# PEER trunk: exponential of the picks written one step later, one-hot compare on pairs, some splits and modulation rows given to GpSimd

## The chip, the cores and the metric

The kernel runs on one core of a Trainium2 chip. The metric is device time in microseconds (us) of one execution; the time before is a median of three runs.

## The reference, cut to what matters

Two layers; each has a mixer (causal pooling beside sliding-window attention) and then an expert network (PEER), both with a norm scaled and shifted by a modulation `mod = silu(c) @ w_ada + b_ada`. T = 256 tokens, D = 1024, 8 heads, 128 x 128 experts, 16 of them picked per token and head:

```python
def peer_ffn(h, wq, subkeys, u, v):
    q = (hf @ wq).reshape(T, PEER_HEADS, 2, D_HALF)
    s = jnp.einsum('thpd,pnd->thpn', q, subkeys)
    top_s, top_i = lax.top_k(s, PEER_TOPK)                       # 16 of 128, twice per head
    cand = top_s[:, :, 0, :, None] + top_s[:, :, 1, None, :]
    best_s, best_j = lax.top_k(cand.reshape(T, PEER_HEADS, 256), PEER_TOPK)
    i1 = jnp.take_along_axis(top_i[:, :, 0], best_j // PEER_TOPK, axis=-1)
    i2 = jnp.take_along_axis(top_i[:, :, 1], best_j % PEER_TOPK, axis=-1)
    expert = i1 * N_KEYS + i2
    gate = jax.nn.softmax(best_s, axis=-1)
    act = gelu(h . u[expert]) * gate
    return act @ v[expert]
```

## The kernel before

The experts are computed densely: every row of U and V is read once per layer, and a gate matrix of zeros and gates, built on chip from the picks, weighs the activations. Weights are float32 and come as tiles of 128 x 1024 (512 KB). Each is split into two float16 parts: ScalarE writes the high part, `activation(hi, r, Copy, scale)` (L86), and VectorE the low part, `r * scale - hi`, in one operation with two inputs (L87). Per layer the expert network reads 16 tiles of wq, 128 tiles of U and 128 of V, in this order.

`Stream` holds the order of all tiles. SP's queue issues the loads (L81), nine tiles ahead of use, into a pool "raw" of five buffers, so that a load waits until a split has freed its buffer; the splits run three tiles ahead, into a pool "hl" of five buffers.

A tile of U is 24 matmuls of 128x256 (`mm_u`, L309): for each of eight slices hi x hhi, hi x hlo, lo x hhi. Two tiles (a pair) fill a PSUM tile "mm", of which there are two buffers, and ScalarE empties it with one Gelu (L828). TensorE can therefore run two pairs ahead of the Gelu.

The generator `picks()` (L672 to L754) yields 68 steps per layer. The loops over the wq tiles and over the first 32 pairs of U tiles call `next(pick)` in between, some two steps per pair. All steps are VectorE's but for one exponential and one copy on ScalarE and four transposes per token tile on TensorE. In order:

- 48 top-16 searches (L666 to L670: MAX8, FIND_INDEX8, MATCH_REPLACE8, MAX8, FIND_INDEX8), and the candidates between them;
- the softmax of the picked scores: the subtraction of the largest (L706), and on ScalarE the Exp (L707), which needs a table load, as does the Gelu behind it;
- integer arithmetic on the candidate numbers (L710 to L723) and the gates' split (L725 to L731);
- for each of two token tiles and two index halves a one-hot compare of 128x2048 float16 (L736), a product (L740) and four halving adds (L744, L746); then the transposes (L752) and the copy (L753).

Modulation rows: `ada_step` reads a 128x1024 tile of w_ada from the same stream, and VectorE multiplies it by a column of `cond` and adds it to `acc_a` (L287; the first row of eight by L285). In layer 0, 24 of them stand between the U tiles, one about every five tiles from tile 12 on.

The program's order is laid down per engine by a scheduler when the kernel is built: each engine runs its instructions in the order listed, so an instruction that waits holds up all behind it on its engine. In the names below `rawt` is a raw tile, `hlt` a split one (its number tells instances apart), `act` the big resident tile that holds the picks' work areas too.

Of the kernel before, what the change touches and what calls it, by code (L numbers as in the profile page):

```python
# [23 lines left out]
L = 2  # L24
# [21 lines left out]
class Arena:  # L46
    """Hands out column ranges of one float32 tile."""
# [15 lines left out]
class Stream:  # L63
    """Weight tiles [128, 1024] in the order of their use; loads and splits run ahead.  An item with a
    fourth field is loaded into a buffer of the splits."""

    def __init__(self, nc, items, raw, hl, ahead_dma, ahead_conv):
# [4 lines left out]
        self.dma_ins = []  # L72
        self.rt, self.ct = {}, {}
# [11 lines left out]
    def split(self, r, scale, hi, lo):  # L85
        self.nc.scalar.activation(hi, r, AF.Copy, scale=scale)  # L86
        self.nc.vector.scalar_tensor_tensor(lo, in0=r, scalar=scale, in1=hi, op0=ALU.mult,  # L87
                                            op1=ALU.subtract)

    def _conv(self, upto):  # L90
        while self.ncv <= min(upto, self.limit, len(self.items) - 1):
# [10 lines left out]
    def get(self, kind):  # L102
        """The next tile: (hi, lo), or the raw tile where the item has no scale."""
# [17 lines left out]
def trunk(ctx, tc, ins, out):  # L121
# [56 lines left out]
    def spread(main, bg, lo, hi):  # L178
        """bg spread evenly between main[lo:hi]."""
# [48 lines left out]
    def rsqrt(out_ap, ss_ap, scale, n):  # L228
        """out = 1/sqrt(ss*scale + EPS): exp(-ln/2), and a Newton step for float32's accuracy."""
# [740 lines left out]
```

## Time and profile before

| quantity | value |
|---|---|
| median of 3 runs | 1781.52 us (1780.1 to 1783.76) |
| profiled execution, first to last instruction | 1780.2 us |
| TensorE matmul busy | 1705.0 us (96%) |
| VectorE busy | 1436.6 us (81%) |
| ScalarE busy | 852.5 us (48%) |
| GpSimd busy | 29.2 us (2%) |
| DMA read | 360.78 MB, 203 GB/s over the span |

Busy time is a sum over instructions of the profiled execution, and the shares are averages over the whole span; the stretch of the picks lies between some 150 and 310 us in layer 0 and 1020 and 1170 us in layer 1. The profile records that execution's own time as its span, 1780.2 us; the runs that give the median were taken apart from it.

### The profile page before, as it was taken

Reading aid. Unit: us, or ns where it says so; the run is one execution under the profiler, and the core shown is the slowest. Engines: PE = TensorE matmul, PEld = TensorE weight load, DVE = VectorE, ACT = ScalarE, POOL = GpSimd, SP = SyncE. Lnnn points to the kernel's source line nnn. Section 1 sums busy time; section 2 is a strip of 40 time slices with the busy share of each in tenths; the row PEclk is TensorE's granted clock in tenths of the full one; section 3 lists DMA queues with packets and bytes.
Section 4 is the critical chain, followed back from the end, with each engine's and each line's share of the span. In section 5 each row is a group of like instructions: output and inputs, shape, how many; then the busy total and the mean of one; then the engine's idle time right before and its main releaser. Section 6 shows DMA issues by size and latency. Waiting matters only on the chain.

```text
span 1780.2 us, 33654 instructions
## 1 busy us (share of the span) xinstructions
PE 1705.0 (96%) x13524; PEld 1212.5 (68%) x13524; DVE 1436.6 (81%) x2587; ACT 852.5 (48%) x1146; POOL 29.2 (2%) x26
## 2 busy tenths in 40 slices
PE   4999989999999999999999998999999999999998
PEld 3758868999997455444458697888999845454443
DVE  6797999578889999877867499945888899986664
ACT  3645544544444444445656353545444444445543
POOL 0210000000000000000000000000000000000000
PEclk9989999999999999999999999999999999999999
DMA  8773456776665555778844144565555555556773
GB/s 315 285 277 120 168 196 220 264 241 207 222 220 187 187 190 199 257 259 314 315 155 154 36 152 163 180 220 201 187 181 188 186 181 183 185 189 213 227 227 126
DMA packets 100190, 364.04 MB, mean 204 GB/s; under 512 B 11680, under 2 KB 11696, under 8 KB 99648
## 3 DMA queue, kind: packets, MB, share of 16 engines
q1 hardware_dynamic: 99648, 361.29, 59.0%
q8 instruction: 106, 1.74, 0.4%
q0 software_dynamic: 384, 0.58, 0.1%
q14 instruction: 52, 0.43, 0.1%
HBM read 360.78 MB, written 1.05 MB: 203 GB/s over the span
## 4 chain that ended last, share of the span: by engine, by line
PE 81%; DVE 13%; DMA 2%; ACT 2%; issue 2%; SPq 0%; DVEq 0%; ACTq 0%
PE acc L327 38%; PE mm L309 34%; DVE hlt L87 4%; PE g L778 2%; PE g L780 2%; DVE act L670 1%; DVE act L668 1%; DVE act L667 1%; DVE act L669 1%; PE acc L319 1%; DMA rawt<-in_wq_dram 1%; DVE act L666 1%; DMA rawt<-in_adar_dram 1%; PE acc L516 1%; PE g L554 1%
## 5 line engine op out<-in xcount | busy, mean ns | idle before, releaser
L309 PE MATMUL mm<-hbuf,hlt 128*128 128x256 f16 x6816 | 767.5, 273 | 20.6 <-ACT act L828 11.1
L86 ACT ACTIVATE hlt<-rawt 128x1024 f16<-128x1024 f32 x544 | 571.4, 1052 | 439.9 <-PE acc L327 179.9
L87 DVE SCALAR_TENSOR_TENSOR hlt<-rawt,hlt 128x1024 f16<-128x1024 f32 x544 | 660.9, 1219 | 122.5 <-ACT hlt L86 117.9
L309 PEld LDWEIGHTS <-hlt 128*128 128x128 f16 x6816 | 662.8, 98 | 102.3 <-DVE hlt L87 13.4
L327 PE MATMUL acc<-hlt,hbuf 128*128 128x512 f16 x3072 | 674.4, 379 | 5.4 <-ACT hbuf L853 5.4
L327 PEld LDWEIGHTS <-hbuf 128*128 128x128 f16 x3264 | 314.9, 98 | 379.8 <-ACT hbuf L853 5.9
L828 ACT ACTIVATE act<-mm 128x512 f32<-128x512 f32 x128 | 76.4, 597 | 174.4 <-PE mm L309 174.4
L853 ACT ACTIVATE hbuf<-act 128x512 f16<-128x512 f32 x128 | 79.0, 626 | 101.4 <-PE acc L327 101.1
L287 DVE SCALAR_TENSOR_TENSOR acc_a<-rawt,cond,acc_a 128x1024 f32<-128x1024 f32 x59 | 75.6, 1282 | 51.1 <-DMA rawt<-in_adar_dram 50.8
L854 DVE TENSOR_TENSOR hbuf<-act,hbuf 128x512 f16<-128x512 f32 x128 | 87.7, 689 | 31.8 <-ACT hbuf L853 31.8
L768 DVE TENSOR_TENSOR lt<-iot,pk 128x1024 f16<-128x1024 f16 x128 | 87.5, 684 | 1.4 <-ACT pk L753 1.4
L783 DVE TENSOR_TENSOR act<-act,g 128x512 f32<-128x512 f32 x128 | 87.0, 680 | 1.7 <-PE g L780 1.7
L774 DVE TENSOR_TENSOR rl<-rt,pk 128x512 f16<-128x512 f16 x128 | 53.8, 421 | 33.7 <-PE g L780 33.1
L778 PE MATMUL g<-rl,lt 128*128 128x64 f16 x1024 | 78.3, 193 | 0.0
L780 PE MATMUL g<-rh,lt 128*128 128x64 f16 x1024 | 78.2, 193 | 0.0
L778 PEld LDWEIGHTS <-lt 128*128 128x128 f16 x1024 | 71.1, 97 | 8.0
L780 PEld LDWEIGHTS <-lt 128*128 128x128 f16 x1024 | 66.3, 97 | 8.0
L87 DVE SCALAR_TENSOR_TENSOR act<-rawt,act 128x1024 f16<-128x1024 f32 x36 | 46.7, 1305 | 19.8 <-ACT act L86 19.8
L770 DVE TENSOR_TENSOR rt<-iot,pk 128x512 f16<-128x512 f16 x128 | 54.2, 424 | 3.9
L86 ACT ACTIVATE act<-rawt 128x1024 f16<-128x1024 f32 x36 | 37.7, 1058 | 39.9 <-DMA rawt<-in_win_dram 31.8
L773 DVE TENSOR_TENSOR rh<-rt,pk 128x512 f16<-128x512 f16 x128 | 53.5, 418 | 0.1
L309 PE MATMUL mm<-hbuf,act 128*128 128x256 f16 x384 | 47.1, 276 | 0.0
(182 smaller groups left out, 911.0 us busy)
## 6 DMA issues: line engine op xcount, KB each, us to landing
rawt<-in_u_dram SPq DMA_DIRECT2D x256, 512.0 KB, 3.9
rawt<-in_v_dram SPq DMA_DIRECT2D x256, 512.0 KB, 3.9
rawt<-in_adar_dram SPq DMA_DIRECT2D x88, 512.0 KB, 4.4
rawt<-in_wq_dram SPq DMA_DIRECT2D x32, 512.0 KB, 4.6
rawt<-in_win_dram SPq DMA_DIRECT2D x20, 512.0 KB, 4.9
rawt<-in_wout_dram SPq DMA_DIRECT2D x16, 512.0 KB, 5.1
hlt<-in_adar_dram SPq DMA_DIRECT2D x8, 512.0 KB, 7.6
act<-in_msk_dram SPq DMA_DIRECT2D x2, 1024.0 KB, 7.9
```

Of the source, the lines that this page charges most:

```text
L86: self.nc.scalar.activation(hi, r, AF.Copy, scale=scale)
L87: self.nc.vector.scalar_tensor_tensor(lo, in0=r, scalar=scale, in1=hi, op0=ALU.mult, op1=ALU.subtract)
L287: last["ada"] = dve.scalar_tensor_tensor(acc, in0=wt, scalar=sc, in1=acc, op0=ALU.mult, op1=ALU.add).ins
L309: pe.matmul(pt, lhsT=a[:, k], rhs=b[:, k], start=n == 0, stop=n == 23)
L327: last["mm"] = pe.matmul(acc[h], lhsT=a, rhs=b[:, h * 512:(h + 1) * 512], start=first and n == 0, stop=end and n == 2).ins
L768: dve.tensor_tensor(out=lt, in0=iot.unsqueeze(1).to_broadcast([P, 4, 128, 2]), in1=pv[0].to_broadcast([P, 4, 128, 2]), op=ALU.is_equal)
L778: pe.matmul(g3[:, t], lhsT=lt[:, t // 2, :, t % 2], rhs=rl[:, t // 2, :, t % 2], start=True, stop=False)
L780: pe.matmul(g3[:, t], lhsT=lt[:, t // 2, :, t % 2], rhs=rh[:, t // 2, :, t % 2], start=False, stop=True)
L783: dve.tensor_tensor(out=av, in0=av, in1=g3.rearrange("p t i -> p i t"), op=ALU.mult)
L828: act_e.activation(act[:, ip_ * 512:(ip_ + 1) * 512], pt, AF.Gelu, scale=1.0 / WS)
L853: tabs.append(act_e.activation(ahi, src, AF.Copy))
L854: dve.tensor_tensor(out=alo, in0=src, in1=ahi, op=ALU.subtract)
```

## The change

Four edits, told in the order of the diff.

1. `Stream.on_pool` names tiles whose low part is made elsewhere: wq tiles 6, 10, 14 and U tiles 2, 6, ... 58 of each layer. For these ScalarE writes the high part as before, then scales the raw tile in place (L89 of the new file), and GpSimd subtracts (L90). VectorE has no part in them.
2. `ada_step` is called with `pool` in the first 32 pairs: ScalarE scales the row's tile (L291 of the new file), GpSimd adds it to `acc_a` (L293); the first row of eight is ScalarE's alone.
3. The two index rows `jh` are written twice as wide, each value twice, so that the compare reads pairs of equal values against pairs of `iot16`, with two packed elements as the innermost step.
4. The Exp is written behind the first compare instead of right behind the subtraction, and the gates' split behind the first token tile's loop.

```diff
+        self.on_pool = set()
...
-    def split(self, r, scale, hi, lo):
+    def split(self, r, scale, hi, lo, pool=False):
         self.nc.scalar.activation(hi, r, AF.Copy, scale=scale)
+        if pool:
+            self.nc.scalar.activation(r, r, AF.Copy, scale=scale)
+            self.nc.gpsimd.tensor_tensor(out=lo, in0=r, in1=hi, op=ALU.subtract)
+            return
...
-                self.split(self.rt.pop(i), scale, hi, lo)
+                self.split(self.rt.pop(i), scale, hi, lo, i in self.on_pool)
...
     st = Stream(nc, items, raw, hl, 9, 3)
+    for kind, rng in (("w", range(6, 16, 4)), ("u", range(2, 60, 4))):
+        at = [i for i, t in enumerate(items) if t[2] == kind]
+        for l in range(L):
+            mine = at[l * len(at) // L:(l + 1) * len(at) // L]
+            st.on_pool |= {mine[n] for n in rng}
...
-            jh = [a.f(256, F16).rearrange("p (h r) -> p h r", h=16) for _ in range(2)]
+            jh = [a.f(512, F16).rearrange("p (n t) -> p n t", t=2) for _ in range(2)]
...
-            act_e.activation(gt, gt, AF.Exp)
             yield
...
-            dve.tensor_tensor(out=jh[0].rearrange("p h r -> p (h r)"), in0=t2, in1=s4, op=ALU.add)
+            twice = [v.unsqueeze(2).to_broadcast([P, 256, 2]) for v in (t2, s4)]
+            dve.tensor_tensor(out=jh[0], in0=twice[0], in1=twice[1], op=ALU.add)
...
-            dve.tensor_tensor(out=jh[1].rearrange("p h r -> p (h r)"), in0=t2, in1=s4, op=ALU.add)
+            dve.tensor_tensor(out=jh[1], in0=twice[0], in1=twice[1], op=ALU.add)
...
-                    j4 = jh[s][:, tt * 8:tt * 8 + 8]
-                    dve.tensor_tensor(out=o1, in0=j4.unsqueeze(3).to_broadcast([P, 8, 16, 16]),
-                                      in1=iot16.unsqueeze(1).unsqueeze(1).to_broadcast([P, 8, 16, 16]),
+                    j4 = jh[s][:, tt * 128:tt * 128 + 128]
+                    dve.tensor_tensor(out=o1.rearrange("p h r (c t) -> p (h r) c t", t=2),
+                                      in0=j4.unsqueeze(2).to_broadcast([P, 128, 8, 2]),
+                                      in1=iot16.rearrange("p (c t) -> p c t", t=2).unsqueeze(1).to_broadcast(
+                                          [P, 128, 8, 2]),
                                       op=ALU.is_equal)
                     yield
+                    if tt == 0 and s == 0:
+                        act_e.activation(gt, gt, AF.Exp)
...
+                if tt == 0:
+                    gate_split()
+                    yield
...
-                    ada_step(pg)
+                    ada_step(pg, pool=ip_ < 32)
```

`gate_split` holds the five lines of the gates' split, unchanged. The number of picks' steps stays 68.

ScalarE's order around the Exp of layer 0. In the order of before, mm_2254 is the Gelu of pair 7, and hlt_2354 and hlt_2395 are the high parts of U tiles 20 and 21:

```order
L828 ACTIVATE act_73<-mm_2178 128x512
L86 ACTIVATE hlt_2319<-rawt_2138 128x1024
L86 ACTIVATE hlt_2348<-rawt_2179 128x1024
L828 ACTIVATE act_73<-mm_2254 128x512
L86 ACTIVATE hlt_2354<-rawt_2185 128x1024
L86 ACTIVATE hlt_2395<-rawt_2214 128x1024
L707 ACT_TABLE_LOAD
L707 ACTIVATE act_73<-act_73 128x256
L828 ACT_TABLE_LOAD
L828 ACTIVATE act_73<-mm_2316 128x512
```

In the order now, mm_2114 is the Gelu of pair 5 (L848), rawt_2077 is a modulation row, rawt_1977 is U tile 14 being scaled in place for GpSimd, and hlt_2194, hlt_2223 and hlt_2290 are the high parts (L87) of U tiles 15, 16 and 17:

```order
L291 ACTIVATE rawt_2077<-rawt_2077,cond_84 128x1024
L89 ACTIVATE rawt_1977<-rawt_1977 128x1024
L87 ACTIVATE hlt_2194<-rawt_2006 128x1024
L848 ACTIVATE act_73<-mm_2114 128x512
L87 ACTIVATE hlt_2223<-rawt_2048 128x1024
L87 ACTIVATE hlt_2290<-rawt_2115 128x1024
L756 ACT_TABLE_LOAD
L756 ACTIVATE act_73<-act_73 128x256
L848 ACT_TABLE_LOAD
L848 ACTIVATE act_73<-mm_2184 128x512
```

The Exp (L707, now L756) moved from behind pair 7's Gelu to behind pair 5's, though it is written later; in layer 1 it moved from pair 6 to pair 5.

VectorE's order behind the Exp of layer 0, at the first compares. Before, hlt_2634 to hlt_2708 are the low parts of U tiles 27 to 30:

```order
L87 SCALAR_TENSOR_TENSOR hlt_2634<-rawt_2460,hlt_2634 128x1024
L736 TENSOR_TENSOR act_73<-act_73,iot16_79 128x2048
L87 SCALAR_TENSOR_TENSOR hlt_2673<-rawt_2489,hlt_2673 128x1024
L740 TENSOR_TENSOR act_73<-act_73 128x2048
L287 SCALAR_TENSOR_TENSOR acc_a_87<-rawt_2606,cond_84,acc_a_87 128x1024
L87 SCALAR_TENSOR_TENSOR hlt_2702<-rawt_2530,hlt_2702 128x1024
L744 TENSOR_TENSOR act_73<-act_73 128x128x8
```

Now (L749 the compare, L757 the product, L92 the low part; hlt_2501 is U tile 23):

```order
L743 CAST act_73<-act_73 128x256
L749 TENSOR_TENSOR act_73<-act_73,iot16_79 128x2048
L744 TENSOR_TENSOR act_73<-act_73 128x256
L757 TENSOR_TENSOR act_73<-act_73 128x2048
L761 TENSOR_TENSOR act_73<-act_73 128x128x8
L761 TENSOR_TENSOR act_73<-act_73 128x128x4
L761 TENSOR_TENSOR act_73<-act_73 128x128x2
L92 SCALAR_TENSOR_TENSOR hlt_2501<-rawt_2324,hlt_2501 128x1024
```

The splits thinned out: the steps of the picks now stand close together, and their last one in layer 0 stands behind the split of U tile 27 instead of 36.

GpSimd's order in the first half of layer 0's U tiles; its list was empty there before. hlt_2008 to hlt_2578 are U tiles 10, 14, 18, 22 and 26, and the lines L293 are modulation rows:

```order
L90 TENSOR_TENSOR hlt_2008<-rawt_1800,hlt_2008 128x1024
L293 TENSOR_TENSOR acc_a_87<-acc_a_87,rawt_2077 128x1024
L90 TENSOR_TENSOR hlt_2187<-rawt_1977,hlt_2187 128x1024
L90 TENSOR_TENSOR hlt_2326<-rawt_2144,hlt_2326 128x1024
L293 TENSOR_TENSOR acc_a_87<-acc_a_87,rawt_2262 128x1024
L90 TENSOR_TENSOR hlt_2471<-rawt_2288,hlt_2471 128x1024
L293 TENSOR_TENSOR acc_a_87<-acc_a_87,rawt_2431 128x1024
L90 TENSOR_TENSOR hlt_2578<-rawt_2402,hlt_2578 128x1024
```

Splits and modulation rows alternate there, all of one shape; before, VectorE had them.

## Rows read from the trace of the kernel before

**Rows 1.** Waits of TensorE's matmuls over the whole span: line, engine and line waited for, us in total, times, longest.

```profile
PE mm L309 <- ACT act L828: 11.1, 2, 6.6
PE mm L309 <- DVE hlt L87: 9.4, 11, 1.7
```

**Rows 2.** Windows: stretch, its length, busy us (instructions) of each engine, granted clock as a share of full speed, busy share of the DMA engines, GB/s. The first two lie in layer 0's picks, the third at layer 1's Exp, the last behind layer 1's picks.

```profile
200.00:250.00 50.00, 45.43 (x406) 38.78 (x404) 49.90 (x216) 20.19 (x23) 0.00 (x0) 1.00 0.58 196
250.00:260.00 10.00, 5.80 (x40) 4.53 (x40) 9.93 (x28) 6.68 (x8) 0.00 (x0) 0.83 0.45 161
1108.00:1123.00 15.00, 8.44 (x57) 6.54 (x56) 14.86 (x46) 6.68 (x8) 0.00 (x0) 0.77 0.30 106
1160.00:1220.00 60.00, 60.00 (x555) 53.79 (x553) 27.90 (x25) 30.38 (x36) 0.00 (x0) 1.00 0.62 214
```

**Rows 3.** Timeline at the Exp of layer 0: start, us, engine, line, operation, shapes, count, and in brackets the idle time before and what ended it.

```profile
251.39 0.41 DVE L706 TENSOR_TENSOR act<-act 128x256 f32<-128x256 f32 x1
251.82 0.42 ACT L707 ACTIVATE act<-act 128x256 f32<-128x256 f32 x1 [8.10 <-DVE act L706]
...
253.55 0.60 ACT L828 ACTIVATE act<-mm 128x512 f32<-128x512 f32 x1
...
254.20 51.80 PE L309 MATMUL mm<-hbuf,hlt 128*128 128x256 f16 x458 [4.54 <-ACT act L828]
```

**Rows 4.** The same at the Exp of layer 1.

```profile
1113.35 0.42 DVE L706 TENSOR_TENSOR act<-act 128x256 f32<-128x256 f32 x1
1113.80 0.42 ACT L707 ACTIVATE act<-act 128x256 f32<-128x256 f32 x1 [9.90 <-DVE act L706]
...
1116.18 14.02 PE L309 MATMUL mm<-hbuf,hlt 128*128 128x256 f16 x106 [6.56 <-ACT act L828]
```

**Rows 5.** A step of the chain of waits in layer 0, behind the picks: start, us, what, matmuls of one pair of U tiles.

```profile
409.61 5.24 PE mm L309 x48
```

**Rows 6.** Timeline of VectorE: a modulation row's first and later operation, a split, and four splits in a row.

```profile
213.59 0.73 DVE L285 TENSOR_SCALAR acc_a<-rawt,cond 128x1024 f32<-128x1024 f32 x1
...
244.32 1.28 DVE L287 SCALAR_TENSOR_TENSOR acc_a<-rawt,cond,acc_a 128x1024 f32<-128x1024 f32 x1
245.52 1.22 DVE L87 SCALAR_TENSOR_TENSOR hlt<-rawt,hlt 128x1024 f16<-128x1024 f32 x1
...
306.41 4.62 DVE L87 SCALAR_TENSOR_TENSOR hlt<-rawt,hlt 128x1024 f16<-128x1024 f32 x4
```

**Rows 7.** Groups by line and form on VectorE: compare and product of layer 0's picks, and the paired compare of the gates over the whole span; busy us, mean ns, idle before.

```profile
L736 DVE TENSOR_TENSOR act<-act,iot 128x2048 f16<-128x2048 f16 x4 | 9.1, 2286 | 0.1
L740 DVE TENSOR_TENSOR act<-act 128x2048 f16<-128x2048 f16 x4 | 4.9, 1216 | 0.0
...
L768 DVE TENSOR_TENSOR lt<-iot,pk 128x1024 f16<-128x1024 f16 x128 | 87.5, 684 | 1.4 <-ACT pk L753 1.4
```

**Rows 8.** The lines L283 and L281, by which GpSimd and ScalarE add and scale modulation rows in the mixer of layer 0: durations in ns (min/median/max), first and last start in us.

```profile
L283 POOL TENSOR_TENSOR grow<-grow,rawt x8: 2346/2354/2966, 51.9 to 102.7; 128x1024 f32<-128x1024 f32 x8
...
L281 ACT ACTIVATE rawt<-rawt,cond x8: 1132/1139/1152, 50.7 to 101.5; 128x1024 f32<-128x1024 f32 x8
```

**Rows 9.** Timeline of layer 0's mixer at three of GpSimd's adds, with VectorE's operations beside them.

```profile
56.58 2.35 POOL L283 TENSOR_TENSOR grow<-grow,rawt 128x1024 f32<-128x1024 f32 x1 [2.34 <-ACT rawt L281]
57.71 2.30 DVE L87 SCALAR_TENSOR_TENSOR act<-rawt,act 128x1024 f16<-128x1024 f32 x1 [0.52 <-ACT act L86]
...
79.05 2.36 POOL L283 TENSOR_TENSOR grow<-grow,rawt 128x1024 f32<-128x1024 f32 x1 [15.25 <-ACT rawt L281]
79.91 1.21 DVE L526 TENSOR_REDUCE act<-act 128x4 f32<-128x1024 f32 x1
...
102.06 1.22 DVE L87 SCALAR_TENSOR_TENSOR act<-rawt,act 128x1024 f16<-128x1024 f32 x1
102.74 2.74 POOL L283 TENSOR_TENSOR grow<-grow,rawt 128x1024 f32<-128x1024 f32 x1 [5.49 <-ACT rawt L281]
103.20 2.37 DVE L357 TENSOR_SCALAR act<-cst,y_r 128x128 f32<-128x128 f32 x1
```

**Rows 10.** Groups by line and form on VectorE in three stretches: the first three rows from layer 0's first search to its L706 (158.20 to 251.38 us), the next two from there to the end of layer 0's picks (299.00 us), the last from layer 1's first search to its L706 (1024.20 to 1113.34 us).

```profile
L87 DVE SCALAR_TENSOR_TENSOR hlt<-rawt,hlt 128x1024 f16<-128x1024 f32 x28 | 33.7, 1206 | 0.0
...
L287 DVE SCALAR_TENSOR_TENSOR acc_a<-rawt,cond,acc_a 128x1024 f32<-128x1024 f32 x2 | 2.5, 1270 | 0.0
...
L285 DVE TENSOR_SCALAR acc_a<-rawt,cond 128x1024 f32<-128x1024 f32 x1 | 0.7, 730 | 0.0
...
L87 DVE SCALAR_TENSOR_TENSOR hlt<-rawt,hlt 128x1024 f16<-128x1024 f32 x16 | 19.4, 1217 | 0.0
...
L287 DVE SCALAR_TENSOR_TENSOR acc_a<-rawt,cond,acc_a 128x1024 f32<-128x1024 f32 x3 | 3.8, 1276 | 0.0
...
L87 DVE SCALAR_TENSOR_TENSOR hlt<-rawt,hlt 128x1024 f16<-128x1024 f32 x27 | 32.5, 1208 | 0.0
```

**Rows 11.** Timeline at the end of layer 0's picks: the split of U tile 36, TensorE's loads of it, and the picks' last add on VectorE.

```profile
296.69 1.22 DVE L87 SCALAR_TENSOR_TENSOR hlt<-rawt,hlt 128x1024 f16<-128x1024 f32 x1
...
297.96 7.75 PEld L309 LDWEIGHTS <-hlt 128*128 128x128 f16 x72 [0.19 <-DVE hlt L87]
298.71 0.39 DVE L746 TENSOR_TENSOR act<-act 128x128 f16<-128x128 f16 x1
```

**Rows 12.** Timeline of layer 0 at one modulation row: two splits, of which the first frees its buffer, the issue of its load, the operation that uses it, and TensorE behind that.

```profile
299.02 2.35 DVE L87 SCALAR_TENSOR_TENSOR hlt<-rawt,hlt 128x1024 f16<-128x1024 f32 x2
...
300.26 0.33 SPq L81 DMA_DIRECT2D rawt<-in_adar_dram  x1
...
305.20 1.28 DVE L287 SCALAR_TENSOR_TENSOR acc_a<-rawt,cond,acc_a 128x1024 f32<-128x1024 f32 x1 [3.83 <-DMA rawt<-in_adar_dram]
...
307.68 4.54 PE L309 MATMUL mm<-hbuf,hlt 128*128 128x256 f16 x40 [1.68 <-DVE hlt L87]
```

More of the change, by code (lines that the diff above doesn't have):

```diff
@@ L722, in picks, with gate_split @@
             dve.tensor_tensor(out=t2, in0=t2, in1=t1, op=ALU.mult)
-            dve.tensor_tensor(out=jh[1].rearrange("p h r -> p (h r)"), in0=t2, in1=s4, op=ALU.add)
+            dve.tensor_tensor(out=jh[1], in0=twice[0], in1=twice[1], op=ALU.add)
             yield
-            dve.tensor_reduce(out=gsum, in_=gt, axis=AX.X, op=ALU.add)
-            dve.reciprocal(gsum, gsum)
-            dve.scalar_tensor_tensor(gt, in0=gt, scalar=GS, in1=gsum.unsqueeze(2).to_broadcast([P, 16, 16]),
-                                     op0=ALU.mult, op1=ALU.mult)
-            gf = gt.rearrange("p h r -> p (h r)")
-            dve.tensor_copy(gp[0], gf)
-            dve.tensor_tensor(out=gp[1], in0=gf, in1=gp[0], op=ALU.subtract)
-            yield
+            def gate_split():
+                dve.tensor_reduce(out=gsum, in_=gt, axis=AX.X, op=ALU.add)
+                dve.reciprocal(gsum, gsum)
+                dve.scalar_tensor_tensor(gt, in0=gt, scalar=GS,
+                                         in1=gsum.unsqueeze(2).to_broadcast([P, 16, 16]),
+                                         op0=ALU.mult, op1=ALU.mult)
+                gf = gt.rearrange("p h r -> p (h r)")
+                dve.tensor_copy(gp[0], gf)
+                dve.tensor_tensor(out=gp[1], in0=gf, in1=gp[0], op=ALU.subtract)
             for tt in range(2):
                 for s in range(2):
-                    j4 = jh[s][:, tt * 8:tt * 8 + 8]
-                    dve.tensor_tensor(out=o1, in0=j4.unsqueeze(3).to_broadcast([P, 8, 16, 16]),
-                                      in1=iot16.unsqueeze(1).unsqueeze(1).to_broadcast([P, 8, 16, 16]),
+                    j4 = jh[s][:, tt * 128:tt * 128 + 128]
[3 more added lines that the diff above has]
+                                          [P, 128, 8, 2]),
                                       op=ALU.is_equal)
                     yield
+                    if tt == 0 and s == 0:
+                        act_e.activation(gt, gt, AF.Exp)
                     dve.tensor_tensor(out=o2, in0=o1,
```

## The prediction

> **What bounds the kernel now.** I read the page's engine shares first, then the waits of TensorE, then windows over the stretch that the change touches, then the timeline there. TensorE waits for little: of its matmul waits only two kinds belong to this stretch, 11.1 us for ScalarE's Gelu and 9.4 us for VectorE's low parts [rows 1]. The windows show where: from 200 to 260 us TensorE is short of work while VectorE is full; from 1160 on, with VectorE half idle, TensorE is full [rows 2]. So inside the picks VectorE is the bound, and outside them nothing the change touches is.
>
> The largest wait is one event per layer. ScalarE's Exp waits for the subtraction of L706, and the next Gelu stands behind it; TensorE, with two "mm" buffers, runs dry until that Gelu is done: 4.54 us in layer 0, 6.56 us in layer 1 [rows 3, 4]. TensorE resumes 2.81 and 2.83 us after L706 starts (254.20 - 251.39; 1116.18 - 1113.35). It then runs slow for a while: a pair of U tiles takes 5.24 us [rows 5], so 458 matmuls would take 50.0 us where 51.80 passed, and 106 would take 11.6 where 14.02 passed [rows 3, 4]: 1.8 and 2.4 us lost. The window of layer 1 shows a granted clock of 0.77, a mixture of the two levels 1.2 and 2.4 GHz behind that wait [rows 2].
>
> **Prices on VectorE.** A split (L87) costs 1.13 us from start to start, (4.62 - 1.22)/3; a modulation row (L287) 1.20; the row L285 0.7 [rows 6]. The compare L736 takes 2.29 us, while 2048 float16 elements with a packed last step take 1.22 (L740) and 1024 in a paired compare 0.684 (L768) [rows 7]. I take 1.22 for the paired compare: four save 4.3 us per layer, if it stays at 2.29 nothing. The two index rows twice as wide cost some 0.5 together, so the picks get 3.8 us shorter.
>
> **Price of GpSimd.** Its add of 128x1024 takes 2.35 us, ScalarE's scaling ahead of it 1.14 [rows 8]. Beside GpSimd, VectorE is held: the split that starts at 57.71, with a GpSimd add running until 58.93, lasts 2.30 us instead of 1.22; the small L357 at 103.20 lasts 2.37, until GpSimd is through, and GpSimd itself waited there for a split that was running (2.74 us). The reduction at 79.91, one input, ran its 1.21 us beside GpSimd unhindered [rows 9]. So an operation with two SBUF inputs that comes up during a GpSimd operation waits for its end, up to 2.35 us; call the mean hold w. No row shows the top-k operations (MAX8 and its kin, one input) beside GpSimd: between the nearest rows, L526 (0) and L357 (2.35), I take 0, since like L526 they run at about an element per clock, and keep both. The Trainium skill ("SBUF — State Buffer", Who interferes with whom) says that an instruction with at most one SBUF input, outside the two-port modes, does not contend with GpSimd; by it that price is zero and the sum stays, by L357's row the second rival below holds.
>
> **Up to the Exp.** The Exp is written later, but the order puts it earlier on ScalarE: in layer 0 behind the Gelu of pair 5 instead of 7, in layer 1 behind pair 5 instead of 6. On VectorE the subtraction stands behind the split of U tile 17 instead of 20 and 19. That is where the relief goes: the scheduler moves picks ahead of splits. Between the first MAX8 and L706 VectorE ran 28 splits, two L287 and one L285 in layer 0, 27 splits in layer 1 [rows 10]; now it runs 19 splits. Layer 0: 9 x 1.13 + 2 x 1.20 + 0.7 = 13.3 us less, so the subtraction starts at 238.1. Seven GpSimd operations fall before it (six in layer 1). The order leaves 5 us of top-k where a split was taken out, longer than 2.35, so I count half a hold here, 1.2 us, and one hold, 2.4, in layer 1 (bounds: none, and all of them full, 16.5 and 14.1). TensorE resumes 2.8 us later, at 242.1, with pair 8; before, it resumed at 254.20 with pair 10, which is 243.7 for pair 8: **-1.6 us**. Layer 1: 1113.35 - 8 x 1.13 + 2.4 + 2.8 = 1109.5 for pair 8, before 1116.18 - 5.24 = 1110.9: **-1.4 us**. The wait for the Exp stays, two pairs and one pair earlier. The slow clock behind it is counted at 1.8 and 2.4 as before.
>
> **Behind the Exp: who is late next.** I test the reckoning on before. In layer 0 VectorE needed from 251.39 to 297.91 for everything up to the split of U tile 36 [rows 11]. TensorE wants that tile eight pairs after 254.20: 41.9 + 2.8 + 1.8 = 46.5 us after L706. Both agree, and TensorE's loads do wait 0.19 us there [rows 11]: VectorE had no slack left. Now the order ends the picks at tile 27 instead of tile 36. Their work: 251.39 to 299.1 is 47.7 us [rows 11], less 16 splits and three L287 [rows 10] (18.1 + 3.6) is 26.0; less 3.8 for the compares, and less 0.7 for two small rows that stand behind tile 27, is 21.5. With the seven splits left on VectorE up to tile 27 (7.9) it needs 29.4 us. TensorE wants tile 27 after 5 x 5.24 + 2.62 + 2.8 + 1.8 = 33.4 us. Without holds it fits. But in layer 0 five GpSimd operations fall in it (splits 18, 22, 26 and two modulation rows), and nearly all of VectorE's operations there have two SBUF inputs: 29.4 + 5 x 2.35 = 41.2, **+7.8 us**. In layer 1 three: 29.4 + 7.1 = 36.5 against 34.0 (2.4 of slow clock), **+2.5 us**. Here w decides: its bounds are 0 and 2.35, and I take 2.35, since the operations that the rows show, splits among them, were held to GpSimd's end.
>
> **Modulation rows.** Before, one row's load, issued when a split freed its buffer (300.26, behind the first of the two splits from 299.02), came late: L287 waited 3.83 us at 305.20 and TensorE 1.68 behind it [rows 12]. VectorE no longer stands there: **-1.7 us**. Now ScalarE waits for that load instead, with a hi part and a Gelu queued behind; a Gelu is wanted two pairs (10.5 us) later, which hides a wait of 4. Behind the Exp this cover is thin: the row whose buffer the split of tile 27 frees would reach ScalarE 41.2 + 4.4 us after the subtraction, and with its scaling (1.14), a hi part (1.05) and the Gelu (0.6) pair 14 could start at 48.4, where TensorE would be there at 41.2 + 2.6. So 0 to 4.6; I take **+2**. From the end of the picks to U tile 63 GpSimd and ScalarE have room, and I cost them at nothing; what hides it is that VectorE is half idle there [rows 2]; if it were not, each operation would cost up to w. No DMA is added; a buffer freed by GpSimd is free some 3 us later, which SP's five buffers (13 us of TensorE) cover. GpSimd's later loads (bias rows, subkeys) stand behind operations that end long before they are wanted.
>
> **Sum.** -1.6 - 1.4 + 7.8 + 2.5 - 1.7 + 2 = +7.6 us on a span of 1780.2: 1787.8. The median of the runs shown, 1781.52, is 1.3 above that span, so the forecast is **1789.1 us**.
>
> **Rivals.** (1) Faster: the holds behind the Exp are short. Most picks there work on float16 alone, and no row shows such an operation beside GpSimd; if those run on and only splits are held, w is about half. It decides at w = 1.3 us: the sum is -1.6 - 1.4 - 1.7 + 2 + (5w - 4.0), with layer 1 fitting below w = 1.5. At w near 0, without the holds before the Exp and the wait for modulation rows, the time is 1781.5 - 1.6 - 1.4 - 3.6 - 1.7 = 1773.2. For it: the type; against it: every two-input operation of rows 9. (2) The top-k operations are held as well: up to 16.5 - 1.2 and 14.1 - 2.4 us more before the Exp, up to 1816. (3) The paired compare is no faster: up to 4.3 us more per layer behind the Exp, 1798. L768 speaks against it. (4) Holds and gains cancel (w near 1.3): 1778 to 1785.
>
> **How the numbers follow.** A measurement of this kernel tells about 0.2% (3.6 us) from no change. Forecast, 1785 to 1797: 0.48. Rival 1 below 1778: 0.26. Rival 4: 0.16. Rivals 2 and 3 with a further loss from slow clock behind more waits: 0.10. So faster 0.26, same 0.16, slower 0.58. The range runs from 1773, rival 1's bound, to 1800: it leaves out what would be gained beyond the bound and most of rival 2. The likeliest case's own range is 1785 to 1797.
>
> **What would show it.** GpSimd's subtract near 2.35 us, and splits or compares of VectorE near 2.3 to 3.5 us beside it; Exp still waited for, TensorE resuming near 242 and 1109; after that waits of TensorE for L92 and for GpSimd's low parts between U tiles 20 and 30 of layer 0, some 10 us together; TensorE full again from there. If VectorE's operations keep their lengths beside GpSimd, the forecast is wrong and rival 1 right; if MAX8 lasts 2 us there, rival 2.

## The result and the profile after

| | before | after |
|---|---|---|
| median, 4 runs each (us) | 1782.19 (1780.1 to 1783.76) | 1793.98 (1792.17 to 1795.35) |
| span of the profiled execution (us) | 1780.2 | 1793.6 |
| VectorE busy (us) | 1436.6 | 1417.0 |
| ScalarE busy (us) | 852.5 | 898.8 |
| GpSimd busy (us) | 29.2 | 141.8 |

The ratio is 1.0055, with a 95% interval of 1.0038 to 1.0072: some 10 us slower (the two medians lie 11.8 apart), where 7.6 were forecast. The profiled execution is the slowest of the four, so the spans differ by more, 13.4 us. VectorE has 20 us less to do, and the kernel is slower.

TensorE's waits in the picks, as in [rows 1] (line, line waited for, us in total, times, longest):

```profile
PE mm L319 <- ACT act L848: 14.6, 5, 6.6
...
PE mm L319 <- POOL hlt L90: 9.9, 4, 3.8
...
PE mm L319 <- DVE hlt L92: 3.2, 3, 1.2
```

Waits for VectorE's low parts fell from 9.4 to 3.2 us; 9.9 us for GpSimd's came instead, and the Gelu's grew by 3.5. The same matmuls in the pages of before and after (busy us, mean ns, idle ahead of them):

```profile
L309 PE MATMUL mm<-hbuf,hlt 128*128 128x256 f16 x6816 | 767.5, 273 | 20.6 <-ACT act L828 11.1
...
L319 PE MATMUL mm<-hbuf,hlt 128*128 128x256 f16 x6816 | 771.9, 274 | 27.7 <-ACT act L848 14.6
```

TensorE stands 7.1 us longer and is busy 4.4 us longer with the same matmuls. The windows that answer to [rows 2]:

```profile
200.00:250.00 50.00, 41.83 (x364) 36.01 (x361) 49.83 (x222) 28.83 (x33) 13.95 (x5) 0.97 0.50 173
250.00:260.00 10.00, 8.72 (x55) 6.63 (x56) 10.00 (x8) 3.86 (x5) 5.96 (x3) 0.66 0.62 211
1108.00:1123.00 15.00, 7.20 (x57) 5.72 (x55) 14.86 (x66) 4.71 (x7) 0.00 (x0) 0.81 0.41 142
1160.00:1220.00 60.00, 60.00 (x552) 53.79 (x550) 25.94 (x18) 35.99 (x40) 11.92 (x6) 1.00 0.63 214
```

From 250 to 260 us VectorE is busy for all 10 us with 8 instructions. Before it had 28, but other ones, the last searches and small operations; that it is held now shows in the next rows. TensorE counts 8.72 us there for 55 matmuls, at a granted clock of 0.66, a mixture of its two levels (1.2 and 2.4 GHz) behind waits of 2.77 and 3.82 us. In the last window GpSimd works for 11.92 us and TensorE is full.

The timeline at the Exp of layer 0 and behind it (start, us, engine, line, operation, tiles, shapes; in brackets the idle time ahead and what ended it):

```profile
239.02 0.42 DVE L716 TENSOR_TENSOR act<-act 128x256 f32<-128x256 f32 x1
...
239.47 0.42 ACT L756 ACTIVATE act<-act 128x256 f32<-128x256 f32 x1 [6.26 <-DVE act L716]
...
241.84 5.62 PE L319 MATMUL mm<-hbuf,hlt 128*128 128x256 f16 x50 [2.77 <-ACT act L848]
...
244.76 6.47 POOL L90 TENSOR_TENSOR hlt<-rawt,hlt 128x1024 f16<-128x1024 f32 x1 [12.60 <-issue]
...
249.16 0.24 DVE L738 RECIPROCAL act<-act 128x16 f32<-128x16 f32 x1
249.33 2.16 DVE L761 TENSOR_TENSOR act<-act 128x256 f16<-128x256 f16 x1
...
251.28 10.94 PE L319 MATMUL mm<-hbuf,hlt 128*128 128x256 f16 x73 [3.82 <-POOL hlt L90]
...
251.40 2.58 DVE L739 SCALAR_TENSOR_TENSOR act<-act 128x256 f32<-128x256 f32 x1
...
253.90 3.14 DVE L92 SCALAR_TENSOR_TENSOR hlt<-rawt,hlt 128x1024 f16<-128x1024 f32 x1
```

The subtraction came at 239.0 (forecast 238.1, and 239.3 with the half hold) and TensorE resumed at 241.84 with pair 8 (242.1). Then GpSimd's low part of U tile 18 took 6.47 us, TensorE waited 3.82 for it, and the next operations of VectorE (L761, L739, L92) were held some 2 us each. Layer 1 repeats it; it starts its first pair 12.0 us later than before, so that 1121.02 is 1109.0 on the clock of before (1109.5 forecast):

```profile
1121.02 7.08 PE L319 MATMUL mm<-hbuf,hlt 128*128 128x256 f16 x50 [6.56 <-ACT act L848]
...
1123.93 6.47 POOL L90 TENSOR_TENSOR hlt<-rawt,hlt 128x1024 f16<-128x1024 f32 x1 [22.92 <-ACT rawt L89]
...
1130.46 5.77 PE L319 MATMUL mm<-hbuf,hlt 128*128 128x256 f16 x36 [2.37 <-POOL hlt L90]
```

Later in layer 0, holds on VectorE beside GpSimd, and ScalarE at a modulation row:

```profile
263.33 3.35 POOL L293 TENSOR_TENSOR acc_a<-acc_a,rawt 128x1024 f32<-128x1024 f32 x1 [7.37 <-ACT rawt L291]
264.50 3.27 DVE L757 TENSOR_TENSOR act<-act 128x2048 f16<-128x2048 f16 x1
...
267.69 3.15 DVE L92 SCALAR_TENSOR_TENSOR hlt<-rawt,hlt 128x1024 f16<-128x1024 f32 x1
...
270.89 10.44 PE L319 MATMUL mm<-hbuf,hlt 128*128 128x256 f16 x94 [0.92 <-DVE hlt L92]
...
277.38 1.22 DVE L92 SCALAR_TENSOR_TENSOR hlt<-rawt,hlt 128x1024 f16<-128x1024 f32 x1
...
282.52 1.15 ACT L291 ACTIVATE rawt<-rawt,cond 128x1024 f32<-128x1024 f32 x1 [6.79 <-DMA rawt<-in_adar_dram]
283.58 1.04 ACT L87 ACTIVATE hlt<-rawt 128x1024 f16<-128x1024 f32 x1
...
284.52 0.57 ACT L848 ACTIVATE act<-mm 128x512 f32<-128x512 f32 x1
...
285.15 17.36 PE L319 MATMUL mm<-hbuf,hlt 128*128 128x256 f16 x146 [3.82 <-ACT act L848]
```

ScalarE stood 6.79 us for a row's load; a high part and the Gelu of pair 12 were queued behind, and TensorE lost 3.82 us. The 94 matmuls from 270.89 end with pair 13; in before the Gelu of that pair shows its end:

```profile
276.87 0.60 ACT L828 ACTIVATE act<-mm 128x512 f32<-128x512 f32 x1 [1.56 <-PE mm L309]
```

The searches aren't held beside GpSimd (0.25 to 0.29 us each in both layers, as without it):

```profile
230.02 2.13 POOL L90 TENSOR_TENSOR hlt<-rawt,hlt 128x1024 f16<-128x1024 f32 x1
...
230.07 0.26 DVE L676 MAX8 act<-act 128x8 f32<-128x112 f32 x1
```

The paired compare L749 costs what a packed operation does, by the groups of 150 to 320 us (busy us, mean ns, idle before); the product L757 shows its one hold in the mean:

```profile
L757 DVE TENSOR_TENSOR act<-act 128x2048 f16<-128x2048 f16 x4 | 6.9, 1730 | 0.1
...
L761 DVE TENSOR_TENSOR act<-act 128x256 f16<-128x256 f16 x4 | 3.3, 832 | 0.1
...
L749 DVE TENSOR_TENSOR act<-act,iot 128x2048 f16<-128x2048 f16 x4 | 4.9, 1219 | 0.1
```

### The profile page after: what moved, and what is told of

Same layout as the page of the kernel before. It is cut to its first block, busy times and chain, and to the rows that moved or that the text cites. A ratio compares the mean times of both kernels' runs of the same rounds, so it can differ in the third digit from the quotient of the medians.

```text
span 1793.6 us, 33669 instructions
## 1 busy us (share of the span) xinstructions
PE 1710.1 (95%) x13524; PEld 1215.2 (68%) x13524; DVE 1417.0 (79%) x2540; ACT 898.8 (50%) x1193; POOL 141.8 (8%) x71
## 4 chain that ended last, share of the span: by engine, by line
PE 83%; DVE 10%; DMA 2%; ACT 2%; issue 2%; POOL 0%; SPq 0%; DVEq 0%; ACTq 0%; POOLq 0%
PE acc L337 39%; PE mm L319 36%; DVE hlt L92 2%; PE g L800 2%; PE g L798 2%; DMA rawt<-in_adar_dram 1%; PE acc L329 1%; PE acc L819 1%; DVE act L680 1%; DVE act L678 1%; PE acc L526 1%; DVE act L677 1%; DVE act L92 1%; PE mm L370 1%; ACT hlt L87 1%
## 5 line engine op out<-in xcount | busy, mean ns | idle before, releaser
L319 PE MATMUL mm<-hbuf,hlt 128*128 128x256 f16 x6816 | 771.9, 274 | 27.7 <-ACT act L848 14.6
L92 DVE SCALAR_TENSOR_TENSOR hlt<-rawt,hlt 128x1024 f16<-128x1024 f32 x508 | 644.9, 1275 | 165.9 <-ACT hlt L87 161.9
L87 ACT ACTIVATE hlt<-rawt 128x1024 f16<-128x1024 f32 x544 | 570.6, 1051 | 392.7 <-PE acc L337 181.2
L319 PEld LDWEIGHTS <-hlt 128*128 128x128 f16 x6816 | 666.1, 98 | 110.4 <-issue 15.5
L848 ACT ACTIVATE act<-mm 128x512 f32<-128x512 f32 x128 | 76.1, 594 | 159.3 <-PE mm L319 159.2
L90 POOL TENSOR_TENSOR hlt<-rawt,hlt 128x1024 f16<-128x1024 f32 x36 | 90.4, 2511 | 333.6 <-ACT rawt L89 283.4
L297 DVE SCALAR_TENSOR_TENSOR acc_a<-rawt,cond,acc_a 128x1024 f32<-128x1024 f32 x50 | 64.2, 1283 | 44.5 <-DMA rawt<-in_adar_dram 44.3
L92 DVE SCALAR_TENSOR_TENSOR act<-rawt,act 128x1024 f16<-128x1024 f32 x36 | 46.6, 1300 | 20.4 <-ACT act L87 20.4
L87 ACT ACTIVATE act<-rawt 128x1024 f16<-128x1024 f32 x36 | 37.7, 1058 | 40.1 <-DMA rawt<-in_win_dram 32.0
```

The source lines that it names most:

```text
L90: self.nc.gpsimd.tensor_tensor(out=lo, in0=r, in1=hi, op=ALU.subtract)
L319: pe.matmul(pt, lhsT=a[:, k], rhs=b[:, k], start=n == 0, stop=n == 23)
L848: act_e.activation(act[:, ip_ * 512:(ip_ + 1) * 512], pt, AF.Gelu, scale=1.0 / WS)
```

## The experiments

Theory at the start: the loss is made behind the Exp, by GpSimd and VectorE shutting each other out and by ScalarE's wait for modulation rows. Rivals: GpSimd costs wherever it runs; the compare or the later Exp cost something themselves; the searches are held too.

The last columns are read from each profiled execution: from the Gelu of pair 0 to that of pair 59, layer by layer, less the same of before (339.37 and 335.88 us). They leave out what varies ahead of the stretch, where layer 0's first Gelu lay anywhere from 191.7 to 200.7 us. Each is of one execution: layer 1, in which e_noada and the changed kernel are written alike, differs by 1.8 us between them.

| run | GpSimd has | ratio to before, 95% interval | layer 0 | layer 1 |
|---|---|---|---|---|
| after | splits, rows | 1.0055 (1.0038 to 1.0072) | +9.96 | +1.47 |
| e_neither | nothing | 0.9998 (0.9985 to 1.0011) | -0.20 | +0.07 |
| e_nosplit | rows | 1.0054 (1.0035 to 1.0072) | +7.89 | -0.06 |
| e_noada | splits | 1.0016 (1.0006 to 1.0027) | +5.40 | -0.30 |
| e_early | splits up to U 14 | 0.9965 (0.9951 to 0.9980) | -2.60 | -2.81 |
| e_skip | splits but U 18, 22, 26 | 0.9978 (0.9965 to 0.9991) | -2.88 | -1.87 |
| e_dummy | as e_early, and 3 idle ones | 0.9999 (0.9987 to 1.0011) | +0.42 | +0.37 |
| e_nosplit_defer1 | rows | 1.0073 (1.0049 to 1.0097) | +17.32 | +0.22 |
| e_nosplit_exp7 | rows | 1.0051 (1.0038 to 1.0063) | +8.69 | -0.91 |
| e_nosplit_row3 | rows | 1.0012 (1.0001 to 1.0022) | +2.80 | 0.00 |
| e_more | 16 early splits | 0.9951 (0.9934 to 0.9969) | -5.82 | -6.51 |
| e_earlyhold | as e_early | 0.9951 (0.9935 to 0.9967) | -2.89 | -5.21 |
| e_morehold | as e_more | 0.9931 (0.9912 to 0.9949) | -5.50 | -7.59 |

All edits are to the changed kernel. 0.1% is 1.8 us.

**e_neither**

```diff
-    for kind, rng in (("w", range(6, 16, 4)), ("u", range(2, 60, 4))):
+    for kind, rng in ():
...
-                    ada_step(pg, pool=ip_ < 32)
+                    ada_step(pg)
```

> The changed kernel without any work for GpSimd: only the paired compare and the Exp written later are left. Theory A (the loss is made by GpSimd's operations behind the Exp and by ScalarE's wait for modulation rows): the order puts the Exp behind pair 7 and pair 6 as before, so TensorE resumes near 254 and 1116; the compares take 1.22 us instead of 2.29, which VectorE gets back, but TensorE waited behind the Exp for only 0.19 and 1.68 us, so 1779 to 1782. Rival B (behind the Exp the picks' length is the bound): all of 2 x 3.8 us, 1774 to 1775. Rival C (writing the Exp later costs something by itself): above 1784.

No change, as theory A had it (1783.55 us; before took 1784.28 beside it). In layer 1 TensorE, once it resumed, ran on as before:

```profile
1114.64 85.61 PE L319 MATMUL mm<-hbuf,hlt 128*128 128x256 f16 x762 [6.57 <-ACT act L848]
```

Nothing waited for the compares there, so making them shorter gains nothing by itself; and the Exp, written one step later, stayed where it was.

**e_nosplit, e_noada**: the first line, or the second, of that edit alone.

> The changed kernel with every split's low part on VectorE; modulation rows stay with ScalarE and GpSimd. Theory A: layer 1 has no work for GpSimd and is as in e_neither; in layer 0 ScalarE still waits for rows' loads with a high part and a Gelu behind, 3 to 6 us of TensorE's time, so 1783 to 1787. Rival (the splits on GpSimd are the whole loss): as e_neither, within 1.5 us.

> The changed kernel with modulation rows back on VectorE; the splits of 36 tiles stay with GpSimd. Theory A: the GpSimd subtraction of U tile 18 is kept waiting by the picks' two-input operations in both layers (6.5 us instead of 2.1, TensorE waits 2 to 4), ScalarE no longer waits for rows: 1785 to 1789. Rival (ScalarE's wait for rows costs nothing that is not there anyway): as the changed kernel, within 2 us, 1792 to 1796.

The rows alone cost 9.6 us, more than theory A allowed. The splits alone cost 2.9: 1787.24, inside its range. The mechanism came only in part as expected. In layer 1 the subtraction of U tile 18 took 6.47 us again, but in layer 0 only 2.18; there those of tiles 22 and 26 were kept out and then held VectorE (here a modulation row, L297), and TensorE waited for the split behind it:

```profile
244.61 2.18 POOL L90 TENSOR_TENSOR hlt<-rawt,hlt 128x1024 f16<-128x1024 f32 x1 [20.33 <-ACT rawt L89]
253.89 4.52 POOL L90 TENSOR_TENSOR hlt<-rawt,hlt 128x1024 f16<-128x1024 f32 x1 [7.10 <-issue]
262.50 4.92 POOL L90 TENSOR_TENSOR hlt<-rawt,hlt 128x1024 f16<-128x1024 f32 x1 [4.09 <-ACT rawt L89]
...
265.36 3.15 DVE L297 SCALAR_TENSOR_TENSOR acc_a<-rawt,cond,acc_a 128x1024 f32<-128x1024 f32 x1
...
270.04 5.41 PE L319 MATMUL mm<-hbuf,hlt 128*128 128x256 f16 x48 [1.75 <-DVE hlt L92]
```

The longest wait there, 3.09 us at 281.90, stands behind the subtraction of U tile 30, which held a split; e_skip has that subtraction too, and a wait of 1.71 us behind it.

**e_early, e_skip**: e_noada, and

```diff
-    for kind, rng in (("w", range(6, 16, 4)), ("u", range(2, 60, 4))):
+    for kind, rng in (("w", range(6, 16, 4)), ("u", range(2, 16, 4))):
```

or, for e_skip, U tiles `[2, 6, 10, 14, *range(30, 60, 4)]`.

> Modulation rows on VectorE, and only wq tiles 6, 10, 14 and U tiles 2, 6, 10, 14 on GpSimd, all of which lie beside the top-16 searches; none behind the Exp. Theory A (searches aren't held by GpSimd, two-input operations are): the searches end three splits earlier, TensorE resumes near 242 to 246 and 1109, no wait for GpSimd follows: 1775 to 1780. Rival (GpSimd costs beside the searches too): 1782 or more.

> As e_early, and U tiles 30, 34, ... 58 of each layer on GpSimd too: of the changed kernel's splits on GpSimd only those of U tiles 18, 22 and 26, behind the Exp, are left out. Theory A (GpSimd costs only beside the two-input operations of the picks): as e_early within 2 us, ratio 0.995 to 0.998, 1775 to 1780. Rival (GpSimd holds VectorE wherever it runs, and that reaches TensorE): 1782 or more.

Beside the searches the splits on GpSimd gain: 6.2 us. In e_early there is no hold behind the Exp, and TensorE runs through (e_early, GpSimd's subtractions and TensorE's timeline):

```profile
L90 POOL TENSOR_TENSOR hlt<-rawt,hlt x14: 2117/2132/2391, 151.8 to 1088.4; 128x1024 f16<-128x1024 f32 x14
```

```profile
247.48 78.93 PE L319 MATMUL mm<-hbuf,hlt 128*128 128x256 f16 x696 [3.08 <-ACT act L848]
```

U tiles 30 to 58 on GpSimd add 0.13% with overlapping intervals: not told from nothing. Between e_skip and e_noada only tiles 18, 22 and 26 differ: 0.38%, 6.8 us.

**e_dummy**: e_early, and for U tiles 18, 22 and 26, whose low parts VectorE makes,

```diff
         self.nc.scalar.activation(hi, r, AF.Copy, scale=scale)
+        if idle:
+            self.nc.gpsimd.tensor_tensor(out=self.spare, in0=self.some, in1=hi, op=ALU.subtract)
```

> As e_early, and GpSimd does three subtractions more per layer, where the changed kernel has the splits of U tiles 18, 22 and 26: same shape and types, started by the high part of the same tile, but into a spare tile that nobody reads; VectorE still makes these tiles' low parts, and the orders of VectorE and ScalarE are those of e_early. It measures the holding of VectorE alone. Theory H (VectorE's two-input operations held by GpSimd are what the splits behind the Exp cost): most of the 6.8 us between e_noada and e_skip shows, ratio to before 0.9995 to 1.002. Theory S (GpSimd, kept out by VectorE, delivers its low part late, and TensorE waits for that): as e_early within 2 us, ratio 0.9955 to 0.9975.

Theory H: 0.34% above e_early, 6.0 us, though TensorE never waits for GpSimd here. The intervals leave some 3 us either way, and in e_noada VectorE has three splits fewer to make, so that the 6.8 us can't be divided into holds and late low parts; that holds alone are enough is shown. The subtractions take up to 4.2 us, and TensorE waits longer for VectorE's low parts. The fences: the idle subtraction (there L89); TensorE's waits in e_dummy (low part L94); the same in e_early.

```profile
L89 POOL TENSOR_TENSOR grow<-x_sb,hlt x6: 2123/2774/4216, 235.2 to 1132.3; 128x1024 f16<-128x1024 f32 x6
```

```profile
PE mm L324 <- DVE hlt L94: 10.7, 14, 1.6
```

```profile
PE mm L319 <- DVE hlt L92: 6.4, 5, 2.4
```

**e_nosplit_defer1, e_nosplit_exp7, e_nosplit_row3** ask what the rows cost. Each is e_nosplit with one instruction of ScalarE queued elsewhere, in this order (`gelus` lists the Gelus, `his` the high parts):

```diff
+                    with tc.issue_after(gelus[ip_ - 1]):
+                        ada_step(pg, pool=True)
...
+                        with tc.issue_after(gelus[7 - l]):
+                            act_e.activation(gt, gt, AF.Exp)
...
+            with tc.issue_after(st.his[-3]):
+                act_e.activation(t, wt, AF.Copy, scale=sc)
```

> As e_nosplit (modulation rows with ScalarE and GpSimd, no splits there), but ScalarE's scaling of a row is queued behind the Gelu of the pair before its own, so that no wait for a row's load stands ahead of an older Gelu. Theory A (the rows' cost of 9.6 us is ScalarE waiting for their loads with Gelus queued behind): at least half comes back, ratio to before 0.999 to 1.002, 1782 to 1788. Rival (the cost is the raw buffer that a row holds longer, or GpSimd's adds holding VectorE): no better than e_nosplit, 1790 or more.

A miss that tells nothing about rows: the edit also changed VectorE's order, which now has a long run of searches between two splits, from 221 to 232 us (e_nosplit has splits at 219.46, 222.03 and 225.91), and TensorE waits for the second (L92, then L319):

```profile
221.21 1.22 DVE L92 SCALAR_TENSOR_TENSOR hlt<-rawt,hlt 128x1024 f16<-128x1024 f32 x1
...
231.98 1.23 DVE L92 SCALAR_TENSOR_TENSOR hlt<-rawt,hlt 128x1024 f16<-128x1024 f32 x1
233.26 2.96 PE L319 MATMUL mm<-hbuf,hlt 128*128 128x256 f16 x13 [7.94 <-DVE hlt L92]
```

> As e_nosplit, but the Exp is queued on ScalarE behind the Gelu of pair 7 in layer 0 and 6 in layer 1, where the kernel before has it (in e_nosplit the order has it one pair earlier in layer 0, though the searches end only about 1 us earlier). Theory A (some 4 of the rows' 9.6 us are that Gelu behind the Exp, the rest ScalarE's wait for loads): ratio to before 1.002 to 1.0035, 1787 to 1791. Rival (the Exp's place doesn't matter, it is all waiting for loads): as e_nosplit, 1.0045 to 1.006.

Theory A fell: the Exp's place changes nothing. ScalarE still stands at the rows' loads, as here just ahead of the searches' end:

```profile
248.54 1.15 ACT L291 ACTIVATE rawt<-rawt,cond 128x1024 f32<-128x1024 f32 x1 [7.55 <-DMA rawt<-in_adar_dram]
```

What the order ahead of the prediction already showed then stood out: ScalarE's scaling of row rawt_2077 is listed ahead of the high parts from rawt_2006 and rawt_2048, while SP's order loads these first:

```
L82 DMA rawt_1977<-in_u_dram 128x1024
L82 DMA rawt_2006<-in_u_dram 128x1024
L82 DMA rawt_2048<-in_u_dram 128x1024
L82 DMA rawt_2077<-in_adar_dram 128x1024
```

ScalarE thus waits for the fourth load while the second and third are there. In the wait shown above, the two loads ahead of the row's had landed at 243.59 and 245.75, and the row's landed at 248.46.

> As e_nosplit, but ScalarE's scaling of a modulation row is queued behind the high part of the U tile that follows the row in the order of loads. In e_nosplit the scaling stands some three tiles ahead of that, so ScalarE waits for a load while the high parts of tiles that were loaded earlier, and a Gelu, are queued behind it; VectorE's order differs from e_nosplit's in a few rows only. Theory A (the rows' cost of 9.6 us is this wait on ScalarE): no wait of ScalarE for rows' loads is left and most of the cost is gone, ratio to before 0.9985 to 1.0020, 1782 to 1788. Rival (GpSimd's adds hold VectorE, or the raw buffer is held longer): as e_nosplit, 1.0040 to 1.0065.

Theory A, in this form: 9.6 us became 2.1. ScalarE's scaling of seven rows from 195 to 330 us, in e_nosplit and then in e_nosplit_row3, where it is L293 (busy us, mean ns, idle before, releasers):

```profile
L291 ACT ACTIVATE rawt<-rawt,cond 128x1024 f32<-128x1024 f32 x7 | 8.1, 1151 | 37.0 <-DMA rawt<-in_adar_dram 30.0 <-DVE act L676 7.0
```

```profile
L293 ACT ACTIVATE rawt<-rawt,cond 128x1024 f32<-128x1024 f32 x7 | 7.9, 1135 | 0.0
```

37.0 us of standing became none. (For 7.0 of them the profile names a search, L676; but the row's load landed at 224.11, and its scaling started at 224.19.) The changed kernel itself has, in the same stretch:

```profile
L291 ACT ACTIVATE rawt<-rawt,cond 128x1024 f32<-128x1024 f32 x7 | 8.0, 1147 | 28.1 <-DMA rawt<-in_adar_dram 21.7 <-DVE act L676 6.4
```

The remaining 2.1 us would fit GpSimd's adds beside the picks; no run takes these apart, and none queues the rows so in the changed kernel itself.

**e_more, e_earlyhold, e_morehold**: e_noada, with the tiles `n % 3 != 0` of wq 6 to 15 and U 0 to 15 for GpSimd (e_more); e_early with

```diff
-                        act_e.activation(gt, gt, AF.Exp)
+                        with tc.issue_after(last["gelu"]):
+                            act_e.activation(gt, gt, AF.Exp)
```

(e_earlyhold); and both (e_morehold).

> As e_early, but two of three tiles beside the searches on GpSimd (wq 7, 8, 10, 11, 13, 14 and U 1, 2, 4, 5, ... 14), 16 per layer instead of 7. Theory A (each split taken from VectorE beside the searches brings the Exp 1.1 us forward): some 8 to 12 us less per layer up to the Exp, of which splits held by GpSimd take some back: 1762 to 1771. Rival (VectorE's work behind the Exp becomes the bound and takes the gain): 1774 to 1779.

> As e_early, with the Exp queued on ScalarE behind the Gelu that was written last ahead of it (pair 23), so that no Gelu waits for the searches. Theory A (VectorE's work is the bound, the Exp's wait turns into waits for splits, and only slack behind the Exp is gained): 1770 to 1776. Rival (the wait for the Exp and the slow clock behind it are a loss of their own): both come back, 1761 to 1766. Rival (no slack at all): 1777 to 1780.

> e_more and the Exp held as in e_earlyhold: no GpSimd behind the searches, two of three tiles with GpSimd beside them, no Gelu behind the searches' end. Theory A (both reliefs act on VectorE's total up to the end of the picks): 3 to 6 us less than e_more, 1768 to 1773. Rival (the Exp's wait is already hidden in e_more, or splits take its place fully): as e_more within 2 us.

e_more gave 1775.15, short of theory A's range and inside the rival's, but not for the rival's reason: the gain is missing ahead of the Exp already. In layer 0 the way from the first search to the subtraction takes 77.6 us against 84.0 in e_skip. That is 6.4 us for ten splits fewer, worth 11.3. VectorE now stands 2.7 us for the searches' scores, which ScalarE copies (L823; the 6.8 below lie ahead of the first search), and the casts and additions for the candidates (L705, L707) are held some 2.2 us longer than in e_skip. One of the casts, an operation with one input, lasted 1.63 us instead of 0.22 beside a subtraction that ran from 207.40 for 2.13 us; so it isn't two-input operations alone that are held.

```profile
DVE act L676 <- ACT act L823: 9.5, 4, 6.8
```

```profile
207.98 1.63 DVE L705 CAST act<-act 128x256 f16<-128x256 uint16 x1
```

Behind the Exp nothing more is lost: counted from the Gelu of pair 0, TensorE takes up pair 8 of layer 0 3.1 us ahead of e_early (241.88 - 200.67 against 247.48 - 5.24 - 197.92, since e_early stands one pair later), and the whole stretch is 3.2 us shorter.

e_earlyhold gave 1774.63, inside theory A's range: the waits for the Gelu are gone, and smaller ones for splits stand in their place. e_morehold, at 1770.88, inside theory A's range too, has the lowest median, 12 us under before. The intervals of e_early and e_earlyhold overlap, and so do those of e_more and e_morehold. TensorE's matmuls by the pages of e_early and e_earlyhold:

```profile
L319 PE MATMUL mm<-hbuf,hlt 128*128 128x256 f16 x6816 | 766.8, 273 | 16.0 <-ACT act L848 9.6
```

```profile
L319 PE MATMUL mm<-hbuf,hlt 128*128 128x256 f16 x6816 | 764.5, 273 | 15.4 <-DVE hlt L92 15.4
```

e_earlyhold stands as long as e_early, 15.4 us against 16.0, but in 17 waits of at most 1.6 us; what it gains is mostly that the same matmuls are busy 2.3 us less. Its granted clock from 240 to 270 us was 1.00, in e_early 0.89. All of TensorE's waits that are left there are for VectorE's splits, and so they are in e_morehold (16 waits, 12.8 us).

## Why the prediction was right, and where its sum was not

All counts below are from the Gelu of pair 0 of a layer (before at 197.41 and 1063.43 us, after at 197.83 and 1075.42), so that they add up to the +9.96 and +1.47 us of the table.

- **The sign and the place** held: the picks, and nothing behind them that can be told from nothing (e_skip).
- **Up to the Exp**, -1.6 and -1.4 us were forecast, and TensorE took up pair 8 2.3 and 1.9 us earlier than before (44.0 us behind that Gelu against 46.3; 45.6 against 47.5). The holds there, half of one and one by the forecast, were 0.5 us on a split at 231.52 and 1.95 on an addition (L707) at 1088.71. Searches beside GpSimd kept their 0.25 to 0.29 us, so rival 2 is out; e_early shows the gain without holds behind the Exp, -2.6 and -2.8 us.
- **The paired compare** costs 1.219 us where 1.22 was taken (rival 3 is out). Alone it gains nothing (e_neither), as the sum had it: its 3.8 us stood only in VectorE's reckoning behind the Exp.
- **Behind the Exp**, the holds: +7.8 and +2.5 forecast, with five and three operations of GpSimd at 2.35 us each. In layer 0 five operations of VectorE were held there (L761, L739, L92, L757 and L92 again), for 1.8 to 2.2 us each, 9.8 in all. Pair 13, with U tile 27, was done 83.5 us behind the first Gelu against 79.5 before: 4.0 us late, so that the way from the Exp to there cost 6.3. VectorE had that tile's split done at 278.60, 39.6 us behind the subtraction, where 41.2 was reckoned and 33.4 would have been in time. Layer 1 lost 3.4 behind the Exp (1.5 + 1.9). Float16 operations are held like the others (L757, 3.27 us), so rival 1 is out. The three splits alone cost 6.8 us in both layers (e_noada against e_skip); holding VectorE, without any late low part, cost 6.0 (e_dummy). What the sum had not: GpSimd is shut out as well, and for more than the one operation that the prediction saw (2.74 us in [rows 9]). Its subtraction needs 2.13 us when free and took 6.47 between VectorE's operations, and TensorE's first wait, 3.82 us, was for that. The Trainium skill ("SBUF — State Buffer", Who interferes with whom) says that issue order and not the operation's shape decides who blocks; the trace agrees, with both sides blocked within 10 us.
- **Modulation rows** is the step that was mis-sized: -1.7 and +2, together +0.3, where +2 was taken from 0 to 4.6. The rest of layer 0's stretch, behind pair 13, cost 5.9 us: TensorE waited 3.82 and 0.33 us for Gelus and 1.92 for a low part of GpSimd's, each with work that ScalarE had queued behind a row's scaling; the granted clock fell again behind that (0.72 from 284 to 290 us), and the 1.68 us of before are gone. Alone the rows measured +9.6 us, and 7.0 on top of the splits (1.0055 against 1.0016); both figures include what the rows' adds held VectorE. The prediction reckoned with one late load behind the Exp and took the rest of the rows at nothing. The runs showed ScalarE standing at six of seven rows from 195 to 330 us, 28.1 us in all (37.0 in e_nosplit), because the scaling was queued ahead of high parts whose loads come first; with the scaling queued behind them the rows alone cost 2.1 us instead of 9.6 (e_nosplit_row3).
- **The slow clock** behind the Exp was counted as before; the further waits brought more of it, 0.66 from 250 to 260 us. By the pages, 4.4 of the 11.4 us of both stretches are the same matmuls running longer, and 7.1 are waits. The 4.4 us lie inside the terms above, which the prediction had built from waits and VectorE's work alone.

So the sum of 7.6 us stands against 11.4 in these two executions (9.8 by the ratio): -4.2 up to the Exp for -3.0, 9.7 behind it in the picks for 10.3 of holds, and 5.9 of rows for 0.3. The holds were right in mechanism and near in size, though part of that time was GpSimd's own lateness. The rows were not, and 1794 lies inside the forecast's 1785 to 1797 because that range had room for an error of this size.

## What to carry to other kernels

Give GpSimd elementwise work only beside VectorE operations that it doesn't hold, here the searches (-6 us); three subtractions per layer beside two-input operations took all of that back. When work moves to an engine that runs ahead, compare its new order with the order of the loads: one instruction that waits for a later load stops everything behind it. A faster operation gains nothing where nobody waits for it.

## What was not expected of the hardware

Between back-to-back two-input operations of VectorE a GpSimd subtraction of 128x1024 stretched from 2.13 to 6.47 us, in both layers alike, while VectorE's own operations kept their lengths until GpSimd got in; then L761 took 2.16 us at 249.33, where the other three of its shape took 0.39 each on average ((4 x 0.832 - 2.16) / 3). In e_nosplit_row3 an add took even 7.50 us instead of 2.35:

```profile
256.38 7.50 POOL L295 TENSOR_TENSOR acc_a<-acc_a,rawt 128x1024 f32<-128x1024 f32 x1 [18.03 <-ACT rawt L293]
```

As an estimate, its end less the time that it needs alone tells when GpSimd got in: 249.10 and 1128.27 us in the two layers, 261.53 in e_nosplit_row3. Each time VectorE's reciprocal, an operation with one input, started 0.06 us later (249.16, 1128.33, 261.59). That is not a rule: the subtraction at 262.50 in e_noada got in, by the same estimate, at 265.29, between two operations with two inputs (L92 and L297).
